# Three inner norms of a two-block kernel, with the sums of squares taken through a block of ones

## The chip, the core and the metric

The kernel runs on one core of a Trainium2 chip. The metric is device microseconds for one execution. TensorE (PE in the profile) multiplies, VectorE (DVE), ScalarE (ACT) and GpSimd (POOL) do the rest, and SyncE (SP) issues the transfers of the weights.

## The reference

256 tokens of width 1024 pass through two blocks. The first has two layers (a convolution beside a gated recurrence; then a multi-scale pooling mixer) and ends in a norm of its own; the second has two mixers side by side and a feed-forward part. Cut to the residual stream and its norms:

```python
def rmsnorm(x, g):   return x * rsqrt(mean(x * x) + 1e-6) * g
def modulate(h, shift, scale):   return h * (1 + scale) + shift

for l in (0, 1):                                        # first block
    h = modulate(rmsnorm(x, norm_g[l]), shift[l], scale[l])
    x = x + gate[l] * mixer[l](h)
x = rmsnorm(x, final_g)
h = modulate(rmsnorm(x, g_mix), mod[0], mod[1])         # second block
x = x + mod[2] * token_mixers(h)
h = modulate(rmsnorm(x, g_ffn), mod[3], mod[4])
x = x + mod[5] * swiglu(h)
return rmsnorm(x, g_final)
```

## The kernel before

The stream X is kept as [128 features, 8 feature tiles, 256 tokens], so a norm's sum over features runs over partitions and goes through TensorE. Every weight arrives as a piece of 128x2048 numbers (L330); ScalarE casts it to a high part (L309) and VectorE takes the low part (L310), and a product is three matmuls of 256 moving columns (L357 to L359). Modulation weights arrive in chunks (L502), of which some are multiplied by TensorE (L515, "w,S") and some by VectorE, whose partial sums `part` go through eight narrow matmuls (L482). Ten buffers of the pool `w` hold pieces and chunks. Instructions are put in order by a scheduler from priorities; ScalarE's table sets are loaded by `table` ahead of functions that need them, or where a function needs another set.

Three norms lie inside the kernel, each between a block's last product and the next block's first: **A** between layer 0 and layer 1, **B** between layer 1 and the second block (where two norms follow one another), and **C** between the mixers and the feed-forward part. At each, `residual` adds eight product tiles to X (L625) and squares X on ScalarE (L632, L637; at A and C in pairs that VectorE adds, L634). TensorE then sums the squares: the squares are the stationary operand, 128 tokens at a time, and one column of ones (at B two columns, ones and final_g squared) moves:

```python
for i in range(2):
    nc.tensor.matmul(ms[:, n * i:n * (i + 1)], s1[:, 128 * i:128 * (i + 1)],
                     ones[:, 0:1] if rhs is None else rhs[:, m, :], ...)
```

That leaves one number per token, by partition. `rstd_of` scales it on VectorE (L417) and raises it to -1/2 on GpSimd (L418); `spread` writes it on the diagonal of two 128x128 tiles (`dg`, L407 and L408) and multiplies these with ones (L411), so that all partitions hold the root of every token. Then `modulate` runs, per feature tile: `xa` on VectorE (L562), `h1h` on ScalarE (L563), `h1l` on VectorE (L564); at B the tiles are h2h and h2l, at C h4h and h4l.

At A and C, TensorE multiplies one weight piece with X scaled but not yet normed (`e1h`, `e1l`, `e4h`, `e4l`: L606, 48 matmuls of 258 columns), and VectorE multiplies these products with the root later; ScalarE copies the root out of its bank for that (`r`, L609). At B, products of the second context (`h2ch`, `h2cl`) stand there. At C, `HOLD` puts four matmuls of 256 columns, whose result nobody reads, between the sums (L653). The norm at the end of the kernel is already taken in another way (`wide`): ones are the stationary 128x128 block and the squares move, 256 columns at a time (L640), so that every partition gets the sum of every token; the root comes from Ln and Exp on ScalarE.

Of the kernel before, what the change touches and what calls it, by code (L numbers as in the profile page):

```python
# [28 lines left out]
HOLD = ((), (), (6, 6, 7, 7))  # L29
# [8 lines left out]
# Layer 0 after its first four pieces: weight pieces in order, with modulation chunks (md) between them; the  # L38
# convolution fills what they leave.
# [15 lines left out]
# Layer 1 likewise: (step, group, half).  # L55
# [7 lines left out]
# The mixers of block 2 likewise.  # L63
# [11 lines left out]
# The feed-forward: pairs of up projections, each pair's down projection one piece later.  # L75
# [11 lines left out]
P = 128  # L87
# [48 lines left out]
def pack(inp):  # L136
# [73 lines left out]
    # the convolution's taps in fours, [feature of 32, tap of four] by [feature tile, four, group of 32]  # L210
# [13 lines left out]
def build(tc, gates, wp, mp, vec, xT, cT, c2T, tok, cst, out, dbg=None):  # L224
# [54 lines left out]
    nc.vector.memset(eps6, 1e-6)  # L279
    mhalf = con.tile([P, 2], F32, name="mhalf")  # L280
# [34 lines left out]
    def halves(raw, width):  # L315
        """A weight piece's parts."""
# [27 lines left out]
    def piece(last=False):  # L344
        """The next weight piece; the ones after it are on their way (fewer behind the last of a layer)."""
# [15 lines left out]
    def mm_w(o, w, x, at, start, stop):  # L361
        """o += w[at].T @ x, in float32 (w and x whole) or in three float32r products of their parts."""
# [5 lines left out]
    def mm_cols(o, w, j, h):  # L368
        """o[128 columns, tokens] over all of D."""
# [3 lines left out]
    def cols2(pc, h):  # L373
        """Two column tiles in one bank."""
# [6 lines left out]
    def toks(o, w, h, s):  # L381
        """o[128 tokens, 256 columns] over all of D."""
# [6 lines left out]
    def mm_rows(banks, pc, x, first, last):  # L389
        """Adds two K tiles (x(k): parts) to all of the 1024 output columns."""  # L390
# [13 lines left out]
    def spread(col):  # L404
        """[128 tokens, 2] -> a bank's [128, 256], the same in all partitions."""
# [8 lines left out]
    def rstd_of(ms, n, eps):  # L414
        """(sum / n + eps) ** -0.5 of [128 tokens, 2] sums, spread over the partitions."""
# [15 lines left out]
    def warm(n):  # L431
        """Keeps the tensor engine's clock up while the first weights arrive."""
# [10 lines left out]
    def mod_part(k):  # L443
        """Shift and scale of layer 0, for 128 features (one mask, both conditions): partial sums by column tile."""
# [23 lines left out]
    def x_vector(block, c, w, part):  # L468
        """One block for x alone: two K tiles' products summed on the vector engine, the partitions' sums at the end."""
# [18 lines left out]
    def mod_groups():  # L488
        """Modulation vectors, a chunk at a time: [feature, column tile, condition] for one or two blocks of 1024 columns."""
# [84 lines left out]
    def token_sums(sums):  # L574
        """The sums over a tile's features, [128 tokens, 2]."""
# [5 lines left out]
    def sumsq_all(xs):  # L581
        """Sums of squares of eight feature tiles, in two tiles of four."""
# [10 lines left out]
    def shift_columns(h, sh):  # L593
        """The shift, as two more columns of the scaled X's parts."""
# [4 lines left out]
    def cols_early(pc, h, rs):  # L599
        """Column tiles from X scaled but not yet normed: [(products over the norm, their shift)]."""  # L600
# [7 lines left out]
        out, r = [], t1("r")  # L608
        nc.scalar.copy(r, rs)  # L609
        for b in banks:  # L610
            t, c = t1("t"), small("c", 1)
            nc.scalar.copy(c, b[:, T:T + 1])
            nc.vector.tensor_tensor(out=t, in0=b[:, 0:T], in1=r, op=ALU.mult)
# [3 lines left out]
    def residual(acc, gate, rhs=None, hold=(), early=None, wide=False):  # L617
# [3 lines left out]
        n = 1 if rhs is None else 2  # L621
        for m in range(8):
            pairs = rhs is None and m < 6
            with tc.high_priority():
# [4 lines left out]
                if pairs:  # L629
                    sq = t2("sq2", (P, 2, T))  # L630
                    s1 = sq if wide and m == 5 else t1("s1")
                    nc.scalar.activation(sq, X[:, m - 1:m + 1, :], AF.Square)  # L632
                    if not (wide and m == 5):
                        nc.vector.tensor_tensor(out=s1, in0=sq[:, 0, :], in1=sq[:, 1, :], op=ALU.add)  # L634
                else:
                    s1 = t1("s1")
                    tables["square"] = nc.scalar.activation(s1, X[:, m, :], AF.Square).ins  # L637
            if wide:
                for s in ([s1[:, 0, :], s1[:, 1, :]] if m == 5 else [s1]):
                    nc.tensor.matmul(ms[:, 0:T], ones, s, start=m == 1, stop=m == 7)  # L640
                continue
            for i in range(2):
                nc.tensor.matmul(ms[:, n * i:n * (i + 1)], s1[:, 128 * i:128 * (i + 1)], ones[:, 0:1] if rhs is None else rhs[:, m, :],
                                 start=m == (1 if rhs is None else 0) and i == 0, stop=m == 7 and i == 1)
# [6 lines left out]
        b = mm_bank()  # L651
        for m in hold:
            nc.tensor.matmul(b[:, 0:T], ones, X[:, m, :], start=True, stop=True)  # L653
        return ms

    lbm, om, omn, e0, e1 = (con.tile([P, 8], F32, name=n) for n in ("lbm", "om", "omn", "e0", "e1"))

    # ------------------------------------------------------------ layer 0
    with ExitStack() as st0:
# [61 lines left out]
        def half_piece(s, g, low):  # L721
            """The high or the low part of half of a piece."""
# [52 lines left out]
        # sigmoid(x) = (1 + tanh(x / 2)) / 2: half of the gates' biases and of the taps that follow one  # L775
# [3 lines left out]
        # 4 * softplus(-lam)  # L779
# [21 lines left out]
        # lower bounds of the forget gates: f = lb + om * (1 + tanh) = lbm + om * tanh  # L801
# [13 lines left out]
        # conv branch  # L815
# [9 lines left out]
        def parts(src):  # L825
            """Two feature tiles as the down projection takes them."""
# [4 lines left out]
        def glu(m, a, g):  # L831
            """Gated input of the convolution for one feature tile, and its taps, which give way to other work."""
# [6 lines left out]
        def shift(m):  # L839
            """[feature of 32, tap of four] on the partitions: a product has four taps."""  # L840
# [6 lines left out]
        def conv(m):  # L847
            """The convolution of one feature tile: its last taps on the tensor engine, the first on the vector engine."""
# [99 lines left out]
        def lru_out(m):  # L948
            """Scans and output gate of two heads; returns the gated output's parts."""
# [17 lines left out]
        def conv_norm():  # L967
            """Layernorm statistics of the conv branch."""
# [548 lines left out]
```

## Time and profile before

| | |
|---|---|
| time, median of 3 runs | 958.51 us (958.29 to 958.64) |
| span of the profiled execution, first to last instruction | 954.3 us |
| granted TensorE clock, mean over the span | 0.984 of full speed |
| TensorE busy | 97% |
| VectorE, ScalarE, GpSimd busy | 69%, 54%, 2% |
| HBM read | 182.23 MB, 192 GB/s over the span |

The profile gives no time of the profiled execution of its own beside the span, so 4.2 us of the median of the runs lie around the span. A busy TensorE can still be slow: the granted clock says at which of its two speeds it ran (1.00 is 2.4 GHz, 0.50 is 1.2 GHz), and the two must be read together.

### The profile page before, as it was taken

What the parts mean: (1) busy time and instruction counts of PE and PEld (TensorE: products, weight loads), DVE (VectorE), ACT (ScalarE), POOL (GpSimd) and SP (SyncE); (2) the same over time, 40 slices, a digit from 0 to 9 for tenths busy, and PEclk for the clock granted to TensorE, in tenths of its full rate; (3) what the DMA queues carried; (4) which work ended last, traced back from release to release, by engine and by line L of the source; (5) the groups of instructions that cost most, each with busy time, mean ns of one, the idle gap of its engine ahead of it and who ended that gap; (6) DMA issues with size and microseconds to landing.
All of it is one profiled execution on the core that took longest, in us unless ns stands there. A gap on an engine that the chain in (4) does not pass through costs nothing. (4 is left out here: it accounts for less than half of the span.)

```text
span 954.3 us, 18243 instructions
## 1 busy us (share of the span) xinstructions
PE 921.4 (97%) x7638; PEld 863.0 (90%) x7638; DVE 661.0 (69%) x1202; ACT 514.6 (54%) x929; POOL 16.7 (2%) x30
## 2 busy tenths in 40 slices
PE   8999999899978999999999999999999999999996
PEld 7876888696878789999999999899999999999996
DVE  4688787795786775878857344989578866555543
ACT  3454869677554454446543335872564663544442
POOL 0000000000000000000000000000000000000000
PEclk9999999999998899999989999999999999999999
DMA  9968573344665685564643363344746367555511
GB/s 367 408 205 308 177 251 112 116 177 177 225 222 211 234 298 183 208 230 178 256 153 136 136 220 139 140 158 178 264 147 251 133 220 255 188 180 181 194 65 45
DMA packets 31890, 189.11 MB, mean 198 GB/s; under 512 B 3552, under 2 KB 8032, under 8 KB 10688
## 3 DMA queue, kind: packets, MB, share of 16 engines
q1 hardware_dynamic: 31248, 185.46, 53.6%
q0 software_dynamic: 560, 2.49, 0.7%
q8 instruction: 60, 0.98, 0.4%
q14 instruction: 22, 0.18, 0.1%
HBM read 182.23 MB, written 1.05 MB: 192 GB/s over the span
## 5 line engine op out<-in xcount | busy, mean ns | idle before, releaser
L310 DVE TENSOR_TENSOR w<-w 128x512 fp32r<-128x512 f32 x460 | 297.8, 686 | 142.5 <-ACT w L309 97.3
L309 ACT CAST w<-w 128x512 fp32r<-128x512 f32 x460 | 255.5, 617 | 155.0 <-DVE w L310 103.8
L359 PE MATMUL mm<-h4h,w 128*128 128x256 f32 x336 | 94.7, 282 | 0.1
L358 PE MATMUL mm<-h4l,w 128*128 128x256 f32 x336 | 94.3, 281 | 0.0
L357 PE MATMUL mm<-h4h,w 128*128 128x256 f32 x336 | 94.2, 281 | 0.0
L358 PE MATMUL mm<-h2l,w 128*128 128x256 f32 x288 | 81.8, 285 | 0.0
L357 PE MATMUL mm<-h2h,w 128*128 128x256 f32 x288 | 81.6, 284 | 0.0
L359 PE MATMUL mm<-h2h,w 128*128 128x256 f32 x288 | 81.5, 284 | 0.0
L359 PE MATMUL mm<-hxh,w 128*128 128x256 f32 x256 | 73.1, 286 | 4.7 <-DVE w L310 4.7
L357 PE MATMUL mm<-hxh,w 128*128 128x256 f32 x256 | 72.7, 284 | 1.2 <-ACT w L309 1.2
L358 PE MATMUL mm<-hxl,w 128*128 128x256 f32 x256 | 72.2, 282 | 0.0
L359 PE MATMUL mm<-h1h,w 128*128 128x256 f32 x240 | 67.8, 283 | 0.0
L357 PE MATMUL mm<-h1h,w 128*128 128x256 f32 x240 | 67.7, 282 | 0.0
L358 PE MATMUL mm<-h1l,w 128*128 128x256 f32 x240 | 67.7, 282 | 0.0
L359 PEld LDWEIGHTS mm<-h4h,w 128*128 128x128 f32 x336 | 63.5, 189 | 0.3 <-DVE w L310 0.3
L358 PEld LDWEIGHTS mm<-h4l,w 128*128 128x128 f32 x336 | 63.4, 189 | 0.0
L357 PEld LDWEIGHTS mm<-h4h,w 128*128 128x128 f32 x336 | 63.2, 188 | 0.0
L358 PEld LDWEIGHTS mm<-h2l,w 128*128 128x128 f32 x288 | 54.3, 189 | 0.3 <-issue 0.2
L359 PEld LDWEIGHTS mm<-h2h,w 128*128 128x128 f32 x288 | 54.3, 189 | 0.2 <-issue 0.2
L357 PEld LDWEIGHTS mm<-h2h,w 128*128 128x128 f32 x288 | 54.3, 188 | 0.3
L357 PEld LDWEIGHTS mm<-hxh,w 128*128 128x128 f32 x256 | 48.2, 188 | 6.9 <-issue 3.8
L359 PEld LDWEIGHTS mm<-hxh,w 128*128 128x128 f32 x256 | 48.4, 189 | 6.6 <-DVE w L310 6.1
(398 smaller groups left out, 2513.0 us busy)
## 6 DMA issues: line engine op xcount, KB each, us to landing
w<-in_wp SPq DMA_DIRECT2D x115, 1024.0 KB, 4.9
w<-in_mp SPq DMA_DIRECT2D x48, 1024.0 KB, 5.4
four<-up SPq DMA_DIRECT2D x32, 142.0 KB, 3.9
w<-in_wp SPq DMA_DIRECT2D x8, 512.0 KB, 10.7
gw<-in_gates SPq DMA_DIRECT2D x4, 512.0 KB, 3.6
X<-in_xT SPq DMA_DIRECT2D x1, 1024.0 KB, 5.3
ct<-in_cT SPq DMA_DIRECT2D x2, 512.0 KB, 9.3
c<-in_c2T POOLq DMA_DIRECT2D x2, 512.0 KB, 6.3
```

The costliest lines, as they stand in the source:

```text
L309: a = nc.scalar.copy(hi, src).ins
L310: return a, nc.vector.tensor_tensor(out=lo, in0=src, in1=hi.bitcast(F32), op=ALU.subtract).ins
L357: nc.tensor.matmul(o, wh, xh, start=start, stop=False)
L358: nc.tensor.matmul(o, wh, xl, start=False, stop=False)
L359: nc.tensor.matmul(o, wl, xh, start=False, stop=stop)
```

## The change

All of `residual` takes the way of the last norm. Ones are stationary, the squares move, six matmuls of 256 columns per norm; the root comes out of `rstd_wide`, Ln and Exp on ScalarE, in all partitions, in SBUF. The narrow sums, GpSimd's power, the diagonals, `spread` at these places, the copy `r` and the four matmuls of `HOLD` go. At B the sums with the weight final_g squared come from squares of X scaled by its root (`weight`), one tile of 256 columns at a time, and the plain sums that the first of the two norms needs are taken apart, in `plain_sums`. Three `table` calls stand ahead of the residuals, and with the functions that follow them ScalarE has six more table loads in all.

```diff
-HOLD = ((), (), (6, 6, 7, 7))
+HOLD = ((), (), ())
...
-        out, r = [], t1("r")
-        nc.scalar.copy(r, rs)
+        out = []
...
-            nc.vector.tensor_tensor(out=t, in0=b[:, 0:T], in1=r, op=ALU.mult)
+            nc.vector.tensor_tensor(out=t, in0=b[:, 0:T], in1=rs, op=ALU.mult)
...
-                    nc.scalar.activation(sq, X[:, m - 1:m + 1, :], AF.Square)
-                    if not (wide and m == 5):
+                    if weight is None:
+                        nc.scalar.activation(sq, X[:, m - 1:m + 1, :], AF.Square)
+                    else:
+                        for j in range(2):
+                            nc.scalar.activation(sq[:, j, :], X[:, m - 1 + j, :], AF.Square, scale=weight[:, m - 1 + j:m + j])
+                    if m < 5:
...
-            if wide:
-                for s in ([s1[:, 0, :], s1[:, 1, :]] if m == 5 else [s1]):
-                    nc.tensor.matmul(ms[:, 0:T], ones, s, start=m == 1, stop=m == 7)
-                continue
-            for i in range(2):
-                nc.tensor.matmul(ms[:, n * i:n * (i + 1)], s1[:, 128 * i:128 * (i + 1)], ones[:, 0:1] if rhs is None else rhs[:, m, :],
-                                 start=m == (1 if rhs is None else 0) and i == 0, stop=m == 7 and i == 1)
+            for s in ([s1[:, 0, :], s1[:, 1, :]] if m == 5 else [s1]):
+                nc.tensor.matmul(o, ones, s, start=m == 1, stop=m == 7)
...
+    def plain_sums():
...
+        for i in range(4):
+            sq, s1 = t2("sq2", (P, 2, T)), t1("s1")
+            nc.scalar.activation(sq, X[:, 2 * i:2 * i + 2, :], AF.Square)
+            nc.vector.tensor_tensor(out=s1, in0=sq[:, 0, :], in1=sq[:, 1, :], op=ALU.add)
+            if i % 2:
+                nc.vector.tensor_tensor(out=s1, in0=s1, in1=sums.pop(), op=ALU.add)
+            sums.append(s1)
+        ms = ms_bank()
+        for i in range(2):
+            nc.tensor.matmul(ms[:, 0:T], ones, sums[i], start=i == 0, stop=i == 1)
+        return ms
+
+    def rstd_wide(ms, bias):
+
+        r = t1("rs")
+        act(r, ms[:, 0:T], AF.Ln, scale=1.0 / D, bias=bias)
+        act(r, r, AF.Exp, scale=-0.5)
+        return r
...
+        table("natural_log_exp_and_others")
         ms = residual(acc, mod_vector("gate0")[:, :, 0], hold=HOLD[0], early=early and (scale1, early))
...
-            rs1 = rstd_of(ms[:, 0:2], D, 1e-6)
...
+            rs1 = rstd_wide(ms, eps6)
...
+        nc.vector.tensor_tensor(out=fg2, in0=v("final_g", 0, 8), in1=v("final_g", 0, 8), op=ALU.mult)
+        nc.vector.tensor_scalar(out=fg2, in0=fg2, scalar1=1e-6, scalar2=None, op0=ALU.add)
+        nc.gpsimd.tensor_tensor(fg2, fg2, half, ALU.pow)
+        table("natural_log_exp_and_others")
...
-            nc.gpsimd.tensor_tensor(vb, vb, mhalf, ALU.pow)
-            rs3 = spread(vb)
-        nc.gpsimd.tensor_tensor(r2, va, mhalf, ALU.pow)
-        rs2 = spread(r2)
+            rs3 = rstd_wide(ms, eps12)
+        rs2 = rstd_wide(plain_sums(), eps6)
```

TensorE's order at norm A, from the last product of layer 0 (`acc<-yh,w`) to the first products of layer 1 (`mm<-h1h,w`); before, the narrow sums (`ms<-ones,s`) stand between early products, and the spread (`ms<-dg`) and the narrow matmuls of `part` behind them:

```order
L359 MATMUL acc<-yh,w 128x256
L643 MATMUL ms<-ones,s_3286 128x1 x2
L606 MATMUL acc<-e1h,w 128x258
L643 MATMUL ms<-ones,s_3294 128x1 x2
L606 MATMUL acc<-e1h,w 128x258 x13
...
L606 MATMUL acc<-e1h,w 128x258 x7
L411 MATMUL ms<-dg,ones 128x128 x2
L482 MATMUL ms<-ones,part 128x1 x8
L606 MATMUL acc<-e1h,w 128x258 x11
L606 MATMUL acc<-e1l,w 128x258 x14
```

Of the same place after the change:

```order
L361 MATMUL acc<-yh,w 128x256
L646 MATMUL ms<-s_3289,ones 128x256
...
L646 MATMUL ms<-s_3311,ones 128x256
L484 MATMUL ms<-ones,part 128x1 x8
L608 MATMUL acc<-e1h,w 128x258 x4
L517 MATMUL ms<-w,S_81 32x512 x12
L608 MATMUL acc<-e1h,w 128x258 x2
L517 MATMUL ms<-w,S_81 32x512 x4
L608 MATMUL acc<-e1h,w 128x258 x10
L525 MATMUL ms<-C,row 128x4 x4
L608 MATMUL acc<-e1h,w 128x258 x8
```

All six sums now stand together behind the last product, the eight narrow matmuls of `part` right behind them, and the modulation chunks (L515 before, L517 now), which stood behind all early products, between these.

TensorE's order at norm B, from layer 1's last product (`acc<-zh,w`) into the second context's products (`mm<-h2ch,w`), before:

```order
L359 MATMUL acc<-zh,w 128x256
L643 MATMUL ms<-fg_5410,s_5415 128x2 x2
L643 MATMUL ms<-fg_5410,s_5420 128x2 x2
...
L643 MATMUL ms<-fg_5410,s_5435 128x2 x2
L357 MATMUL mm<-h2ch,w 128x256
L358 MATMUL mm<-h2cl,w 128x256
```

And after:

```order
L361 MATMUL acc<-zh,w 128x256
L646 MATMUL ms<-s_5409,ones 128x256
L646 MATMUL ms<-s_5417,ones 128x256
L646 MATMUL ms<-sq_5424,ones 128x256 x2
L359 MATMUL mm<-h2ch,w 128x256
L646 MATMUL ms<-s_5430,ones 128x256
L646 MATMUL ms<-s_5434,ones 128x256
```

Ten narrow matmuls of the first five tiles stood together (six more follow between context products); now the six wide ones stand there with one context product among them, and the two of the plain sums come 16 and 23 context products later.

ScalarE's order at B after the change, from the squares scaled by `fg` to the first modulated tile (`h2h`); before, eight squares and no other work of the norm stood here but two diagonals:

```order
L638 ACTIVATE sq_5424<-X,fg_5398 128x256 x2
L664 ACTIVATE sq_5440<-X 128x512
L664 ACTIVATE sq_5444<-X 128x512
L644 ACTIVATE s_5430<-X,fg_5398 128x256
L644 ACTIVATE s_5434<-X,fg_5398 128x256
L664 ACTIVATE sq_5449<-X 128x512
L664 ACTIVATE sq_5453<-X 128x512
L294 ACTIVATE rs<-ms,eps_76 128x256
L311 CAST w<-w 128x512
L294 ACTIVATE rs<-rs 128x256
```

Two of the four plain squares come ahead of the last two weighted ones, and two between these and the Ln that reads their sum.

## Rows read from the trace of the kernel before

**Rows 1.** The page: TensorE's busy time, and its granted clock in 40 slices.

```profile
PE 921.4 (97%) x7638; PEld 863.0 (90%) x7638; DVE 661.0 (69%) x1202; ACT 514.6 (54%) x929; POOL 16.7 (2%) x30
PEclk9999999999998899999989999999999999999999
```

**Rows 2.** Stretches: us; busy PE, PEld, DVE, ACT, POOL; clock, DMA share, GB/s.

```profile
306.00:314.00 8.00, 8.00 (x70) 8.00 (x70) 5.92 (x16) 5.68 (x13) 0.34 (x1) 1.00 1.01 424
314.00:324.00 10.00, 9.16 (x50) 8.78 (x48) 7.51 (x19) 5.35 (x12) 0.52 (x1) 0.66 0.39 163
492.00:504.00 12.00, 12.00 (x65) 12.00 (x65) 3.95 (x10) 3.36 (x8) 2.67 (x4) 0.57 0.25 88
746.00:758.00 12.00, 11.84 (x94) 11.43 (x93) 9.57 (x27) 8.11 (x21) 0.88 (x1) 1.00 0.25 93
944.00:947.00 3.00, 2.34 (x11) 1.71 (x9) 2.24 (x8) 2.22 (x6) 0.00 (x0) 1.00 0.00 0
580.00:590.00 10.00, 10.00 (x86) 10.00 (x86) 4.08 (x7) 4.34 (x8) 0.00 (x0) 1.00 0.32 111
590.00:630.00 40.00, 37.35 (x308) 35.77 (x308) 39.49 (x74) 35.61 (x59) 1.07 (x2) 1.00 0.36 131
```

**Rows 3.** Timeline of TensorE at A: start, us, operation, count, wait before.

```profile
309.41 0.50 PE L643 MATMUL ms<-ones,s 128*128 128x1 f32 x4
...
314.99 0.68 PE L411 MATMUL ms<-dg,ones 128*128 128x128 f32 x4 [0.66 <-DVE dg L407]
315.51 3.14 PE L482 MATMUL ms<-ones,part 128*128 128x1 f32 x16
...
324.62 3.64 PE L515 MATMUL ms<-w,S 128*32 128x512 f32 x32
...
331.21 0.36 PE L357 MATMUL mm<-h1h,w 128*128 128x256 f32 x1
```

**Rows 4.** Timelines of ScalarE, GpSimd and VectorE at A.

```profile
310.62 0.71 ACT L637 ACTIVATE s<-X 128x256 f32<-128x256 f32 x2
...
313.66 0.86 POOL L418 TENSOR_TENSOR rs<-rs,mhalf 128x2 f32<-128x2 f32 x1 [110.10 <-DVE rs L417]
...
315.71 1.26 DVE L562 SCALAR_TENSOR_TENSOR xa<-X,a,ms 128x256 f32<-128x256 f32 x3
```

**Rows 5.** Timelines of TensorE and ScalarE at B.

```profile
491.09 2.29 PE L643 MATMUL ms<-fg,s 128*128 128x2 f32 x20
...
511.71 0.28 PE L359 MATMUL mm<-h2h,w 128*128 128x256 f32 x1
...
492.43 0.81 ACT L637 ACTIVATE s<-X 128x256 f32<-128x256 f32 x2 [0.23 <-DVE X L625]
```

**Rows 6.** Timelines of TensorE and VectorE at C.

```profile
747.57 0.51 PE L643 MATMUL ms<-ones,s 128*128 128x1 f32 x4
...
756.25 2.09 PE L606 MATMUL acc<-e4l,w 128*128 128x258 f32 x16
...
754.69 1.26 DVE L562 SCALAR_TENSOR_TENSOR xa<-X,a,ms 128x256 f32<-128x256 f32 x3
```

**Rows 7.** Timelines of TensorE and ScalarE in the last norm.

```profile
944.45 1.03 PE L640 MATMUL ms<-sq,ones 128*128 128x256 f32 x4
...
945.32 1.03 PE L640 MATMUL ms<-s,ones 128*128 128x256 f32 x4
946.38 0.47 ACT L292 ACTIVATE rs<-ms,eps 128x256 f32<-128x256 f32 x1 [0.41 <-PE ms L640]
946.89 0.42 ACT L292 ACTIVATE rs<-rs 128x256 f32<-128x256 f32 x1
```

**Rows 8.** Timeline of TensorE elsewhere: narrow matmuls of another `part`.

```profile
687.68 1.62 PE L482 MATMUL ms<-ones,part 128*128 128x1 f32 x14
```

**Rows 9.** ScalarE's table loads, grouped, and the timeline around one.

```profile
L292 ACT ACT_TABLE_LOAD x22 | 28.2, 1283 | 1.1 <-DVE lx L1263 0.7
...
588.48 0.60 ACT L292 ACTIVATE sg<-mm 128x512 f32<-128x512 f32 x1 [1.05 <-PE mm L359]
```

More of the change, by code (lines that the diff above doesn't have):

```diff
@@ L279, in build @@
     nc.vector.memset(eps6, 1e-6)
+    eps12 = con.tile([P, 1], F32, name="eps12")
+    nc.vector.memset(eps12, 1e-12)
     mhalf = con.tile([P, 2], F32, name="mhalf")
@@ L612, in cols_early, with residual @@
             nc.scalar.copy(c, b[:, T:T + 1])
-            nc.vector.tensor_tensor(out=t, in0=b[:, 0:T], in1=r, op=ALU.mult)
+            nc.vector.tensor_tensor(out=t, in0=b[:, 0:T], in1=rs, op=ALU.mult)
             out.append((t, c))
         return out
-    def residual(acc, gate, rhs=None, hold=(), early=None, wide=False):
+    def residual(acc, gate, weight=None, hold=(), early=None):
         ms = ms_bank()
-        n = 1 if rhs is None else 2
+        o = ms[:, 0:T]
         for m in range(8):
-            pairs = rhs is None and m < 6
+            pairs = m < 6
             with tc.high_priority():
@@ L630, in residual @@
                     sq = t2("sq2", (P, 2, T))
-                    s1 = sq if wide and m == 5 else t1("s1")
-                    nc.scalar.activation(sq, X[:, m - 1:m + 1, :], AF.Square)
-                    if not (wide and m == 5):
+                    s1 = sq if m == 5 else t1("s1")
+                    if weight is None:
[4 more added lines that the diff above has]
+                    if m < 5:
                         nc.vector.tensor_tensor(out=s1, in0=sq[:, 0, :], in1=sq[:, 1, :], op=ALU.add)
@@ L636, in residual @@
                     s1 = t1("s1")
-                    tables["square"] = nc.scalar.activation(s1, X[:, m, :], AF.Square).ins
-            if wide:
-                for s in ([s1[:, 0, :], s1[:, 1, :]] if m == 5 else [s1]):
-                    nc.tensor.matmul(ms[:, 0:T], ones, s, start=m == 1, stop=m == 7)
-                continue
-            for i in range(2):
-                nc.tensor.matmul(ms[:, n * i:n * (i + 1)], s1[:, 128 * i:128 * (i + 1)], ones[:, 0:1] if rhs is None else rhs[:, m, :],
-                                 start=m == (1 if rhs is None else 0) and i == 0, stop=m == 7 and i == 1)
+                    kw = {} if weight is None else {"scale": weight[:, m:m + 1]}
+                    tables["square"] = nc.scalar.activation(s1, X[:, m, :], AF.Square, **kw).ins
+            for s in ([s1[:, 0, :], s1[:, 1, :]] if m == 5 else [s1]):
+                nc.tensor.matmul(o, ones, s, start=m == 1, stop=m == 7)
         if early:
@@ L650, in residual @@
                                                in1=h[0][:, m, 0:T].bitcast(F32), op0=ALU.mult, op1=ALU.subtract)
-        b = mm_bank()
-        for m in hold:
-            nc.tensor.matmul(b[:, 0:T], ones, X[:, m, :], start=True, stop=True)
-        return ms
+        if hold:
+            b = mm_bank()
+            for m in hold:
+                nc.tensor.matmul(b[:, 0:T], ones, X[:, m, :], start=True, stop=True)
+        return ms
+    def plain_sums():
+        sums = []
+        for i in range(4):
[14 more added lines that the diff above has]
+        return r
     lbm, om, omn, e0, e1 = (con.tile([P, 8], F32, name=n) for n in ("lbm", "om", "omn", "e0", "e1"))
@@ L1152, in build @@
         nc.vector.tensor_tensor(out=fgA, in0=fgA, in1=v("final_g", 0, 8), op=ALU.mult)
-        fg2 = con.tile([P, KT, 2], F32, name="fg2")
-        nc.vector.memset(fg2, 1.0)
-        nc.vector.tensor_tensor(out=fg2[:, :, 1], in0=v("final_g", 0, 8), in1=v("final_g", 0, 8), op=ALU.mult)
+        fg2 = con.tile([P, KT], F32, name="fg2")
+        half = con.tile([P, KT], F32, name="half")
+        nc.vector.memset(half, 0.5)
+        nc.vector.tensor_tensor(out=fg2, in0=v("final_g", 0, 8), in1=v("final_g", 0, 8), op=ALU.mult)
+        nc.vector.tensor_scalar(out=fg2, in0=fg2, scalar1=1e-6, scalar2=None, op0=ALU.add)
+        nc.gpsimd.tensor_tensor(fg2, fg2, half, ALU.pow)
+        table("natural_log_exp_and_others")
         ms = residual(acc, mod_vector("gate1")[:, :, 0], fg2, HOLD[1])
@@ L1158, in build @@
         tap("x2", X)
-        mv = ms[:, 0:4].rearrange("p (i n) -> p i n", n=2)
-        va, vb, r2 = small("va"), small("vb"), small("r2")
-        nc.vector.tensor_scalar(out=va, in0=mv[:, :, 0], scalar1=1.0 / D, scalar2=1e-6, op0=ALU.mult, op1=ALU.add)
-        nc.vector.tensor_scalar(out=vb, in0=va, scalar1=1e-6, scalar2=None, op0=ALU.mult)
-        nc.vector.scalar_tensor_tensor(out=vb, in0=mv[:, :, 1], scalar=1.0 / D, in1=vb, op0=ALU.mult, op1=ALU.add)
         with tc.high_priority():
-            nc.gpsimd.tensor_tensor(vb, vb, mhalf, ALU.pow)
-            rs3 = spread(vb)
-        nc.gpsimd.tensor_tensor(r2, va, mhalf, ALU.pow)
-        rs2 = spread(r2)
+            rs3 = rstd_wide(ms, eps12)
+        rs2 = rstd_wide(plain_sums(), eps6)
         hx = [h_tile("h2h", "hxh"), h_tile("h2l", "hxl")]
@@ L1445, in build @@
             shift_columns(early, shift3)
+        table("natural_log_exp_and_others")
         ms = residual(acc, gate2, hold=HOLD[2], early=early and (scale3, early))
@@ L1448, in build @@
         with tc.high_priority():
-            rs4 = rstd_of(ms[:, 0:2], D, 1e-6)
+            rs4 = rstd_wide(ms, eps6)
     hx = [h_tile("h4h", "hxh"), h_tile("h4l", "hxl")]
@@ L1480, in build @@
     table("natural_log_exp_and_others")
-    ms = residual(acc, mod_vector("gate3")[:, :, 0], wide=True)
-    rs5 = t1("rs5")
+    ms = residual(acc, mod_vector("gate3")[:, :, 0])
     with tc.high_priority():
-        act(rs5, ms[:, 0:T], AF.Ln, scale=1.0 / D, bias=eps6)
-        act(rs5, rs5, AF.Exp, scale=-0.5)
+        rs5 = rstd_wide(ms, eps6)
     for m in range(8):
```

## The prediction

> **What bounds the kernel now.** I read the page first, then the busy time and clock by stretch, then the timelines of the three norms. The page says that TensorE is busy 97% of the span [rows 1], so time can come from three sources only: work that TensorE no longer does, moments in which it waits, and stretches in which it is busy at a lower clock. The clock line of the page shows 8 in place of 9 in two pairs of slices, around 310 and around 490 us [rows 1]. The stretches put numbers on them. At A the clock is 1.00 until 314 and 0.66 on the mean of the ten microseconds after it; at B it is 0.57 on the mean of the twelve from 492 [rows 2]. These are losses that busy shares hide: at B TensorE counts as busy for 12.00 of 12.00 us. At C the clock stays at 1.00 [rows 2].
>
> What did TensorE do before each fall? At B, twenty records of matmuls with two moving columns from 491.09 on, 2.2 us of them and nothing else, and the clock is down behind them [rows 2, 5]. At A, narrow sums among early products, a wait of 0.66 us for the diagonals, then sixteen records with one column, already slow at 3.14 us [rows 3]; fourteen of the same kind take 1.62 elsewhere [rows 8]. At C the narrow sums alternate with products, four of them kept for that. So what stands before a fall is narrow work by itself, with or without a wait. Narrow matmuls count as busy but do little.
>
> **The change, norm by norm.** I place TensorE's list of instructions after the change at full clock, add the waits, and compare the ends. Prices of one record or matmul: 0.13 us for an early product (16 in 2.09) [rows 6], 0.12 for a product of 256 columns (86 in 10 us) [rows 2], 0.43 for a wide sum (two in 0.87, since each has two records) [rows 7], 0.115 for a narrow one (14 in 1.62) [rows 8], 0.114 for one of a modulation chunk (32 in 3.64) [rows 3].
>
> A. The last product ends at 309.41 [rows 3]. Six wide sums: 2.6 us, to 312.0. The last square is done at 310.62 + 0.71 = 311.33 [rows 4], before the sixth sum would start, so no wait. Then sixteen records for `part`, 1.85, to 313.9. Then all that stands ahead of layer 1's products: 48 early products, 6.2; forty chunk records, 4.55; eight small ones for the chunks' rows, at the same price 0.9. That ends at 325.6. Before, these products run steadily from 331.21 on [rows 3], with nine of them done earlier, which is 330.1 if they had all been behind. Gain: 4.5 us. The parts bear it out: clock (1 - 0.66) x 10 = 3.4, idle 10 - 9.16 = 0.84 [rows 2]; the sums themselves and the diagonals make the rest. Can the norm keep up? Before, the power ends at 314.52, and `xa` starts at 315.71 [rows 4]. After, Ln and Exp end about 1.0 us behind the sums (0.47 and 0.42 with small gaps [rows 7]), at 313.0; `xa` waits a little longer, because the gate vector from `part` is ahead of it on VectorE, until about 314.1. Sixteen VectorE operations at 0.4 us then end near 321, ahead of 325.6. The chunks that now come earlier in TensorE's order are the other thing late: the queue is full until 314 (DMA share 1.01) and at 0.39 on the mean of the ten after that [rows 2], and the first chunk is wanted at 314.4. I take no wait; by one transfer's time, up to 2.5 us (1 MB at 424 GB/s), could go here. A gives between 1.0 (the dip stays) and 4.8; I take 4.5.
>
> B. From 491.09 to the end of the last product of the first two pieces at 511.83 it takes 20.7 us [rows 5]. After: 96 products at 0.12 make 11.5, eight wide sums 3.5, together 15.0. Waits: squares with a scale per column can't be paired, as they were not before either, but two plain squares stand ahead of the last two. These were done at 492.43 + 0.81 = 493.24 [rows 5]; two squares of double length, about 1.4 us by the rate of two in 0.71 [rows 4], less casts that moved, put them near 494.0, where TensorE wants them at 493.4. I add 0.9 us for that and for the second plain sum. End: 507.0, gain 4.8. The clock alone is (1 - 0.57) x 12 = 5.2 [rows 2]; the wide sums cost a little less than the narrow ones and the diagonals, and the new waits take more back. The norm: Ln at about 495.5 behind the last plain squares, Exp done by 497, `xa` from 497.1 instead of 504.1; sixteen VectorE operations and a few weight splits end by 505.5, ahead of the last products at 506.3. Bounds: 5.7 without waits; -0.4 where the dip stays.
>
> C. From 747.57 six wide sums, 2.6, then 48 early products, 6.24: 756.4, and 0.2 of waiting for the last squares, 756.6. Before, the last early product ends at 756.25 + 1.95 = 758.2 [rows 6]. Gain 1.6. `xa` starts at 754.69 before [rows 6]; it will start about 2.4 us earlier, so a few tenths of waiting for modulated tiles go too: I take 1.7, with 1.6 to 2.1 as bounds. No dip is there to win.
>
> **Table loads.** Six more, 1.28 us each (28.2 for 22) [rows 9], 7.7 us of ScalarE. Five are hidden by TensorE's own work: those ahead of the squares at A, B and C run while TensorE still multiplies the block's last pieces, those before layer 1's first gate and before the second block's first forget gates while it multiplies the piece that these read or the next. Without that cover each costs its 1.28. One is on a path: before `sg` at 588.48 ScalarE idles 1.05 [rows 9], so the load pushes it by 0.23, into a stretch in which VectorE is busy 39.49 of 40 us and TensorE 37.35 [rows 2]. I charge 0.2; uncovered, all six would cost 7.7. The Trainium skill ("ScalarE: Activation LUTs", section "What ACT_TABLE_LOAD costs") puts a switch at about 2.66 us with a drain beside the load; by it six switches would be 16 us. The trace has 1283 ns for the load itself [rows 9], and I go by that.
>
> Sum: 4.5 + 4.8 + 1.7 - 0.2 = 10.8. The span of 954.3 becomes 943.5; with the 4.2 us around it that the median shows, 947.7.
>
> **The rivals.**
>
> One dip stays. At A the narrow records of `part` stand right behind the sums, alone, as in the rows before a fall. At 687.68 the same kind ran at full speed, which speaks against it [rows 8]. Price 3.4: 951.1. At B new waits of 0.9 us stand among the sums; price 5.2: 952.9. The Trainium skill ("TensorE: Matmul & The Clock Gate", section "Why this matters for your kernels") blames idle gaps between bursts of matmuls for such falls. At B before no gap shows, 12.00 of 12.00 us are busy, and the clock fell all the same [rows 2]; by that rule narrow matmuls aren't the cause, the change removes no cause at B and even adds a gap, and the time is this rival's 952.9.
>
> Wide sums lower the clock as narrow ones did, at all three norms. This ends on the other side: A gives 1.1, B -0.4, and C, where the kept products are gone, gets a dip that it doesn't have, 3.4 to 5.2, against its 1.7. With the load's 0.2 that is a loss of 1.2 to 3.0: 959.7 to 961.5. It decides from a dip at C of 2.2 us on. Against it: in the last norm, with waits between wide sums (2.34 busy of 3.00), the clock shows 1.00 [rows 2].
>
> Table loads are on the path after all, each at its 1.28: 947.7 + 7.5 = 955.2. Against it: ScalarE is busy 54% [rows 1].
>
> The gain is given back further down: if VectorE's full stretch from 590 to 630 ended when it does now, A and B would be worth nothing and the time 957.0. But VectorE is busy 4.08 of the 10 us ahead of it [rows 2], so the stretch starts when TensorE brings its products, and moves with them.
>
> **How the numbers follow.** Forecast 0.62; one dip stays 0.17; three dips 0.06; loads 0.06; given back 0.05; 0.04 for what I don't see. The forecast's own range is 945 to 950 (the bounds of the three norms, and one late chunk). The range of 944.5 to 955.5 takes in one dip and the loads, and leaves out some 0.15. Faster or slower by 0.2%, 1.9 us, is about what a measurement of this kernel can tell from no change. Faster: forecast, one dip, most of the loads, part of the rest, 0.87. Within: given back, 0.05. Slower: three dips and unseen things, 0.08.
>
> **What would show it.** The clock at 1.00 through 305 to 325, and through a stretch of 20 us from about 486 on; layer 1's products steady near 325.6 on a clock of before, and B's end some 9 us earlier than 511.8; wide sums at 0.43 each; Ln right behind the sixth; `xa` at C near 752 less the shift. A time over 950 with the clock at 1.00 would mean waits that I haven't placed, for chunks at A or for ScalarE at B; a clock under 1.00 at any of the three would show narrowness was not the cause, or not alone.

## The result, and the profile after

The changed kernel takes 944.7 us (median of 4 runs, 941.7 to 946.9) against 958.4 us before (4 runs, 956.5 to 958.6); ratio 0.9865, 95% interval 0.9837 to 0.9893. Measured a second time it was 944.7 against 954.8 us (0.9891, 0.9867 to 0.9916). The ratios are given as recorded; the quotient of two medians differs from them a little (0.9857 in the first measurement). The prediction was 947.7 us, 944.5 to 955.5, so the measured time lies 0.2 us above the lower end of its range. The two gains, 13.7 and 10.2 us, are the same measurement twice, and the difference between them is a part of the story: the times of the kernel before go from 951.0 to 957.9 us in the second measurement, at mean clocks of 0.991 to 0.980 of full speed, and those of the changed kernel from 943.4 to 945.8 at 0.992 to 0.988. One of the five runs of the kernel with a fill, below, took 1475.6 us at a mean clock of 0.555 and is left out of that kernel's times.

The page of the changed kernel, TensorE's busy time and its clock, answers to [rows 1]:

```profile
PE 909.1 (97%) x7582; PEld 851.2 (91%) x7582; DVE 660.4 (70%) x1201; ACT 525.6 (56%) x941; POOL 15.0 (2%) x27
PEclk9999999999998999999999999999999999999998
```

One of the two low places, near 490 us, is gone. The other has shrunk to one slice, which belongs to something else, at 288 us. The 8 in the last slice stands where TensorE has no work left. Stretches of the changed kernel (columns as in [rows 2]):

```profile
306.00:314.00 8.00, 8.00 (x60) 6.02 (x62) 7.08 (x20) 6.18 (x15) 0.00 (x0) 1.00 1.01 422
314.00:324.00 10.00, 10.00 (x85) 6.93 (x74) 8.29 (x21) 7.01 (x15) 0.00 (x0) 1.00 0.56 193
484.00:500.00 16.00, 16.00 (x120) 15.21 (x119) 14.56 (x36) 13.72 (x30) 0.99 (x2) 1.00 0.19 67
735.00:747.00 12.00, 12.00 (x92) 11.54 (x91) 12.00 (x31) 11.53 (x29) 0.00 (x0) 1.00 0.26 87
282.00:288.00 6.00, 1.18 (x8) 0.98 (x6) 4.36 (x8) 5.73 (x12) 0.00 (x0) 0.84 0.71 269
288.00:296.00 8.00, 8.00 (x50) 7.99 (x50) 3.53 (x7) 5.06 (x8) 0.00 (x0) 0.69 0.00 0
```

The first two rows are A, the third B, the fourth C: TensorE is busy all the time and at full clock, where before it was at 0.66 and 0.57 behind A and B [rows 2]. The last two rows show a wait ahead of A, for the conv branch, and the dip behind it (a stretch at a low clock), which the change doesn't touch.

TensorE's timeline at A, B and C, with the rows that answer to [rows 3], [rows 5] and [rows 6]:

```profile
307.22 1.12 PE L646 MATMUL ms<-s,ones 128*128 128x256 f32 x4
...
309.20 1.14 PE L646 MATMUL ms<-s,ones 128*128 128x256 f32 x4
310.18 1.84 PE L484 MATMUL ms<-ones,part 128*128 128x1 f32 x16
...
484.80 1.02 PE L646 MATMUL ms<-s,ones 128*128 128x256 f32 x4
485.66 1.03 PE L646 MATMUL ms<-sq,ones 128*128 128x256 f32 x4
486.74 1.13 PE L646 MATMUL ms<-s,ones 128*128 128x256 f32 x4
489.63 0.59 PE L671 MATMUL ms<-s,ones 128*128 128x256 f32 x2
...
500.37 0.39 PE L387 MATMUL mm<-w,h2h 128*128 128x256 f32 x1 [0.27 <-ACT kx L294]
...
735.58 1.02 PE L646 MATMUL ms<-s,ones 128*128 128x256 f32 x4
...
737.30 1.05 PE L646 MATMUL ms<-s,ones 128*128 128x256 f32 x4
738.01 4.22 PE L608 MATMUL acc<-e4h,w 128*128 128x258 f32 x32
742.06 2.08 PE L608 MATMUL acc<-e4l,w 128*128 128x258 f32 x16
```

The sums follow the last product without a wait at all three; the row at 500.37 is the first behind the products that end B. The chain of the norm at A, on ScalarE and VectorE, and the last weighted squares at B:

```profile
310.38 0.47 ACT L294 ACTIVATE rs<-ms,eps 128x256 f32<-128x256 f32 x1 [0.39 <-PE ms L646]
310.88 0.42 ACT L294 ACTIVATE rs<-rs 128x256 f32<-128x256 f32 x1
...
312.06 0.17 DVE L486 TENSOR_TENSOR gate<-ms,V 128x8 f32<-128x8 f32 x1 [0.92 <-PE ms L484]
312.14 1.26 DVE L564 SCALAR_TENSOR_TENSOR xa<-X,a,rs 128x256 f32<-128x256 f32 x3
...
486.19 0.89 ACT L644 ACTIVATE s<-X,fg 128x256 f32<-128x256 f32 x2
```

The root is there 1.1 us behind the sums; `xa` waits 0.8 us more for the gate vector ahead of it on VectorE, as foreseen, and nothing waits for `xa`.

For all comparisons below, the length of a norm runs from the end of the block's last product (0.12 us behind the start of its last record) to a point behind it with the same number of products done: at A the start of the fortieth record of layer 1's products, at B the end of the first two pieces, at C the start of the sixtieth record of the feed-forward's. "Dip" is the loss of a stretch at a low clock: the sum of (1 - clock) times length over stretches of 4 us. Each kernel was profiled in one execution (the changed kernel in two). The ratio is to the kernel before, measured beside it; the kernel before has a median from each of the two measurements.

| kernel | A, us | B, us | C, us | dips at A, B, C, us | median, us | ratio to before |
|---|---|---|---|---|---|---|
| before | 25.4 | 20.7 | 18.0 | 3.4, 5.1, 0 | 958.4; 954.8 | |
| changed | 21.3 | 15.1 | 15.5 | 0, 0, 0 | 944.7 | 0.9865 |
| changed, again | 21.0 | 15.1 | 15.5 | 0, 0, 0 | 944.7 | 0.9891 |
| A alone | 21.0 | 19.3 | 18.0 | 0, 3.4, 0 | 950.6 | 0.9961 |
| B alone | 25.3 | 15.1 | 18.0 | 3.4, 0, 0 | 952.1 | 0.9962 |
| C alone | 25.4 | 20.8 | 15.5 | 3.4, 5.1, 0 | 951.7 | 0.9965 |

Between the norms nothing changed: from A to B 156.2 us in every row of this table, from B to C 235.4 to 235.7.

### The profile page after: what moved, and what is told of

It is laid out like the page before. It is cut to its first block, busy times and chain, and to the rows that moved or that the text cites. A ratio compares the mean times of both kernels' runs of the same rounds, so it can differ in the third digit from the quotient of the medians.

```text
span 939.6 us, 18146 instructions
## 1 busy us (share of the span) xinstructions
PE 909.1 (97%) x7582; PEld 851.2 (91%) x7582; DVE 660.4 (70%) x1201; ACT 525.6 (56%) x941; POOL 15.0 (2%) x27
## 4 chain that ended last, share of the span: by engine, by line
PE 83%; DVE 7%; ACT 6%; DMA 2%; issue 1%; SPq 0%; POOL 0%; DVEq 0%; ACTq 0%; POOLq 0%
PE mm L359 16%; PE mm L361 16%; PE mm L360 16%; PE acc L359 7%; PE acc L360 6%; PE acc L361 6%; PE acc L762 2%; PE ms L517 2%; PE acc L884 2%; PE acc L608 1%; ACT L294 1%; PE ms L646 1%; DVE w L312 1%; ACT w L311 1%; DMA w<-in_wp 1%
## 6 DMA issues: line engine op xcount, KB each, us to landing
w<-in_wp SPq DMA_DIRECT2D x8, 512.0 KB, 10.8
```

## The experiments

**The changed kernel again, and one norm at a time.** Four kernels on one chip. In three of them the sums, the root and their use at two of the norms are put back as they were; for "A alone":

```diff
-        table("natural_log_exp_and_others")
-        ms = residual(acc, mod_vector("gate1")[:, :, 0], fg2, HOLD[1])
+        ms = residual_n(acc, mod_vector("gate1")[:, :, 0], fg2, HOLD[1])
...
-            rs3 = rstd_wide(ms, eps12)
-        rs2 = rstd_wide(plain_sums(), eps6)
+            nc.gpsimd.tensor_tensor(vb, vb, mhalf, ALU.pow)
+            rs3 = spread(vb)
...
-            rs4 = rstd_wide(ms, eps6)
+            rs4 = rstd_of(ms[:, 0:2], D, 1e-6)
```

(`residual_n` is `residual` of the kernel before.)

> The changed kernel once more, for the spread of its times. The theory (the sums no longer lower the clock at A and B) expects the granted clock at 1.00 through all three norms in this execution too, and places the spread of 941.7 to 946.9 us outside the norms: in a dip that comes or stays away where TensorE idles for some microseconds (near 172 and 286 us). The rival (one dip stays in some executions, behind the narrow matmuls of part at A or the waits among the sums at B) expects, in a slow-ish execution, a clock under 1.00 between 306 and 324 or between 484 and 500 us. Time 942 to 947.

> The change at norm A alone. Theory: clock 1.00 at A, 0.57 still at B, A worth 3.9 to 4.5 us, the time 0.40 to 0.47% under before. Rival (the clock is lost by idle moments, not by narrow work): only the wait for the diagonals goes, A worth about 1 us.

> The change at norm B alone. Theory: clock 1.00 at B, 0.66 still at A, B worth 4.8 to 5.5 us, 0.50 to 0.58% under before. Rival (idle moments): B had no idle moment before and has some now, so the dip stays and B is worth 0.7 us at most.

> The change at norm C alone, where the clock was at 1.00 before. Theory: 1.7 to 2.2 us from the kept products and the shorter chain, 0.18 to 0.23% under before, dips at A and B as before. Rival (wide sums lower the clock too, once the kept products are gone): a dip behind 747 us and no gain.

Stretches around the norms, first of the changed kernel again (A, then B):

```profile
306.00:324.00 18.00, 18.00 (x140) 13.49 (x140) 16.69 (x44) 14.04 (x31) 0.00 (x0) 1.00 0.86 347
484.00:504.00 20.00, 19.73 (x151) 18.85 (x150) 18.57 (x45) 16.80 (x37) 0.99 (x2) 1.00 0.28 95
```

A alone (A, then B):

```profile
309.00:325.00 16.00, 16.00 (x124) 11.56 (x122) 13.95 (x36) 11.47 (x26) 0.00 (x0) 1.00 0.75 303
488.00:500.00 12.00, 12.00 (x77) 11.98 (x78) 5.35 (x15) 4.30 (x10) 2.68 (x4) 0.72 0.23 85
```

B alone (A, then B):

```profile
316.00:328.00 12.00, 11.12 (x70) 9.51 (x72) 9.83 (x24) 6.37 (x16) 0.30 (x1) 0.72 0.31 128
492.00:508.00 16.00, 16.00 (x120) 15.12 (x118) 14.57 (x36) 13.73 (x30) 0.99 (x2) 1.00 0.19 66
```

C alone (A, B, C):

```profile
316.00:324.00 8.00, 8.00 (x43) 8.00 (x44) 6.12 (x16) 4.05 (x9) 0.00 (x0) 0.57 0.35 145
492.00:508.00 16.00, 16.00 (x100) 15.98 (x99) 7.73 (x19) 6.19 (x15) 2.68 (x4) 0.68 0.19 66
745.00:760.00 15.00, 15.00 (x117) 14.55 (x116) 15.00 (x38) 14.55 (x34) 0.00 (x0) 1.00 0.32 120
```

The clock is at 1.00 at a norm where the sums are wide, and under it at A and B where they are narrow, without an exception in these profiles. The single gains by median, 4.3, 2.8 and 3.1 us (by ratio 3.7, 3.6 and 3.3, each within some 1.9), add up to the whole within their intervals, so no dependence between the norms shows. In the profiled executions A gives 4.1 to 4.5, B 4.1 to 5.6 and C 2.5 us. Part of the expectations missed. B alone came out 0.38% under before instead of 0.50 to 0.58, and C alone 0.35 instead of 0.18 to 0.23, each with an interval of some 0.2 either way. The clock's "0.57" at B is 0.72 over its stretch of 12 us in A alone, because the dip there cost 3.4 and not 5.1 us. So the dips at the same narrow sums differ between executions, and with them the gain. The rival that blames idle moments alone falls with B alone: no wait stood there before, and the dip is gone. At A the change takes away two things at once, narrow sums and a wait of 0.66 us for the diagonals [rows 3]; which of them brought the dip there was not tested apart.

**Does narrow work bring a dip?** Ten narrow matmuls, twenty records of two columns as before at B, whose result nobody reads, were put into the changed kernel, first ahead of the sums at B, then behind them; then twenty ahead of them; then ten in the middle of the feed-forward.

```diff
+            if weight is not None and m == 1:
+                fill = mm_bank()
+                for j in range(10):
+                    nc.tensor.matmul(fill[:, 2 * j:2 * j + 2], s1[:, 0:128], ones[:, 0:2], start=True, stop=True)
             for s in ([s1[:, 0, :], s1[:, 1, :]] if m == 5 else [s1]):
```

(Behind the sums: the same lines after this loop, with `m == 7`. Twenty: `range(20)`. In the feed-forward: with X as the stationary block, behind the ninth piece's products.)

> The changed kernel, with ten narrow matmuls (twenty records of two columns, 2.2 us, result unread) ahead of the first wide sum at B; they lie partly in moments in which TensorE waits there. Theory: the dip of 3.4 to 5.1 us comes back behind them, B takes 19 to 22 us instead of 15.1, and the time is 0.4 to 0.7% over the changed kernel. Rival (idle moments, not narrow work): B takes 16 to 17.3 us, 0.1 to 0.2% over.

Ahead of the sums, the row of the train and the stretch with all of B:

```profile
485.78 2.29 PE L648 MATMUL mm<-ones,s 128*128 128x2 f32 x20
...
485.00:504.00 19.00, 19.00 (x147) 18.45 (x147) 15.97 (x39) 14.57 (x32) 1.05 (x2) 1.00 0.16 56
```

No dip: B takes 17.5 us, 2.3 more than 15.1, which is the train itself; 946.8 us, ratio 0.9907 (0.9890 to 0.9925). The theory as I had put it, that narrow work by itself lowers the clock, missed here.

> The changed kernel with the ten narrow matmuls (twenty records of two columns, 2.2 us, result unread) behind the last wide sum at B, so that context products of 256 columns follow them, as in the kernel before; ahead of the sums they had brought no dip. Theory in its first form (narrow work of 2.2 us by itself lowers the clock, and wide sums behind it had hidden that): the clock falls behind them, B takes 15.1 + 2.2 + 3.4 to 5.1 = 20.7 to 22.4 us, 0.6 to 0.8% over the changed kernel. Rival (a train of this length alone is not enough): B takes 17.3 us, 0.2% over.

Behind the sums:

```profile
490.20 2.29 PE L650 MATMUL mm<-ones,s 128*128 128x2 f32 x20
...
487.00:505.00 18.00, 17.89 (x136) 16.86 (x135) 14.56 (x35) 13.52 (x30) 0.98 (x2) 1.00 0.17 59
```

Again none: B 17.5 us, 947.0 us, ratio 0.9923 (0.9893 to 0.9952). In these two profiles a train of 2.2 us beside wide sums cost about its own length and no more.

> The changed kernel with twenty narrow matmuls (forty records, 4.3 us) in place of ten ahead of the first wide sum at B. Theory in a weaker form (narrow work lowers the clock, but it takes more of it than 2.2 us when wide sums follow): a dip at B of 1.7 to 5.1 us, B 21 to 24.5 us, 0.6 to 1.0% over the changed kernel. Rival (narrow matmuls do not lower the clock at all): B 19.4 us, 0.45% over, the clock at 1.00.

Twice as long, ahead of the sums:

```profile
488.72 5.38 PE L648 MATMUL mm<-ones,s 128*128 128x2 f32 x40
...
488.00:500.00 12.00, 12.00 (x68) 10.99 (x67) 4.75 (x11) 4.72 (x11) 1.05 (x2) 0.72 0.25 89
```

Here the dip is back, 3.4 us, with TensorE busy for 12.00 of 12.00 us; B takes 23.0 us and the run 951.3 (0.9982, 0.9957 to 1.0006). The train alone takes 5.38 us where two of 2.29 would be 4.58, so the clock fell while it ran. So narrow work does lower the clock, without any wait, and forty records did at this place what twenty did not.

> The changed kernel with the ten narrow matmuls (twenty records of two columns, 2.2 us, one stationary block, result unread) in the middle of the feed-forward products, far from any wide sum: products of 256 columns on both sides, as around the narrow sums of the kernel before at B. Beside the wide sums such a train had brought no dip. Theory (a train of 2.2 us lowers the clock among products; the wide sums of twice the time per column beside it had held it up): a dip of 1.7 to 5.1 us behind it, 3.9 to 7.3 us or 0.4 to 0.8% over the changed kernel. Rival (such a train is not enough wherever it stands, and something else of the sums at B brought the dip there): 2.2 us, 0.23% over, the clock at 1.00.

Ten in the feed-forward, the train and the two stretches behind it:

```profile
817.47 2.29 PE L1497 MATMUL ms<-ones,X 128*128 128x2 f32 x20
...
818.00:822.00 4.00, 4.00 (x31) 4.00 (x31) 2.77 (x6) 1.61 (x5) 0.00 (x0) 0.85 0.76 264
822.00:826.00 4.00, 4.00 (x28) 4.00 (x27) 0.00 (x0) 1.02 (x2) 0.00 (x0) 0.72 0.00 0
```

A dip, but a short one: (1 - 0.85) x 4 + (1 - 0.72) x 4 = 1.7 us. The median is 948.1 us, ratio 0.9907 (0.9886 to 0.9929), with single times from 943.8 to 948.7; in this kernel C also took 1.6 us longer, in part because TensorE waited for VectorE among the sums there (0.28 and 0.56 us). Among products the same ten matmuls can bring a dip that they did not bring beside wide sums. One profile and six times don't say how often. One difference between all these trains and the sums of the kernel before stays untested: there, behind the twenty records, twelve more stand in three groups of four among the context products, inside the dip. The first group:

```profile
495.06 0.85 PE L643 MATMUL ms<-fg,s 128*128 128x2 f32 x4
```

**Wide work between the narrow sums.** The kernel before, with a wide matmul, unread, behind each of the first five narrow pairs at B:

```diff
+            if rhs is not None and m < 5:
+                if m == 0:
+                    fill = mm_bank()
+                nc.tensor.matmul(fill[:, 0:T], ones, X[:, m, :], start=True, stop=True)
```

> The kernel before, with five wide matmuls of 0.43 us, whose result nobody reads, one behind each of the first five pairs of narrow sums at B. Theory (narrow work by itself lowers the clock): the clock stays at 1.00 at B, so that B takes 20.7 - 5.1 + 2.2 = 17.8 us or a little more, with the extra work in it; the time is 0 to 0.3% under before. Rival (the narrow sums are not the cause): the dip stays, B takes 22.9 us and the time is 0.2% over before.

The stretch of B, the last narrow sums in it, and its one wait:

```profile
489.00:510.00 21.00, 19.81 (x161) 19.36 (x160) 15.28 (x38) 10.27 (x26) 2.68 (x4) 1.00 0.15 51
...
494.38 1.40 PE L643 MATMUL ms<-fg,s 128*128 128x2 f32 x12
...
498.87 1.16 PE L411 MATMUL ms<-dg,ones 128*128 128x128 f32 x8 [1.19 <-DVE dg L407]
```

The narrow sums are all still there, and the clock stays at 1.00. B takes 19.5 us, 1.2 less than before with 2.2 us of added work; 1.19 us go to the wait for the diagonals, which products at half the speed had hidden, as I read it. Twelve narrow records stand together even so, at 494.38, and bring no dip. The time stays the same (955.8 us, 1.0014, 0.9996 to 1.0032), not the 0 to 0.3% under before that I expected: in the profiled execution a dip of 3.4 us stood near 628 us, where none was before; whether the other eleven had it is not known. So at B of the kernel before the dip hangs on the twenty narrow records standing together, and the chain through GpSimd and the diagonals is the second price. What the whole kernel gains from parting them is not shown by this run.

**The kept products at C.** The kernel before with `HOLD = ((), (), ())`.

> The kernel before without its four kept products at C: ten narrow pairs there stand among early products by ones and twos only. If short trains are harmless (as at B of the changed kernel with ten narrow matmuls ahead): clock 1.00 at C, C 17.9 - 1.7 = 16.2 us or a little more where TensorE then waits, the time 0.1 to 0.2% under before. If the kept products held the clock: a dip of 1.7 to 3.4 us behind the sums, C 18 to 20 us, the time 0 to 0.2% over before.

```profile
744.00:764.00 20.00, 18.76 (x154) 18.19 (x153) 16.55 (x42) 14.78 (x34) 0.87 (x1) 1.00 0.22 68
```

The clock stays at 1.00 without them, C takes 17.6 instead of 18.0 us, and TensorE idles for 1.24 us of the twenty; 954.5 us, ratio 0.9994 (0.9971 to 1.0018). The kept products filled moments in which TensorE would have waited for the norm. At C the gain is thus mostly the chain: without a shorter chain, dropping them is worth 0.4 us of the 2.5 there, and nothing that shows in the whole time.

**Table loads on the path.** The changed kernel without its three `table` calls ahead of the residuals.

```diff
-        table("natural_log_exp_and_others")
         ms = residual(acc, mod_vector("gate1")[:, :, 0], fg2, HOLD[1])
```

> The changed kernel without its three table calls: the loads then stand right ahead of Ln and of Exp, in the chain of the norm (2.6 us more at A and C, 5.1 at B). Theory (at A and C the norm has slack behind the early products; at B it has little): A unchanged within 0.5 us, C 0 to 1 us longer, B 2 to 4 us longer, the time 0.2 to 0.5% over the changed kernel. Rival (the chain of the norm sets the end at all three): 10 us, 1.1% over.

ScalarE's loads at B, then TensorE's wait and its stretch:

```profile
493.68 1.28 ACT L294 ACT_TABLE_LOAD   x1
494.98 0.42 ACT L294 ACTIVATE rs<-rs 128x256 f32<-128x256 f32 x1
...
499.87 0.58 PE L359 MATMUL mm<-h2h,w 128*128 128x256 f32 x1 [3.96 <-ACT h2h L565]
...
496.00:508.00 12.00, 8.13 (x47) 8.13 (x48) 9.25 (x24) 6.79 (x12) 0.00 (x0) 0.72 0.00 0
```

In the profile A is unchanged (20.5), C 2.4 longer, B 6.7 longer (21.9); the median is 949.2 us, 0.9945 (0.9925 to 0.9964), half a per cent over the changed kernel. At A the loads hide behind the early products, as expected; at B four of them make TensorE wait 3.96 us, and with that wait the clock falls, which costs 3.4 more. Neither the theory's 2 to 4 us at B nor the rival's 10 us in all had this second part, and C missed the theory's 0 to 1 us. The profiled execution was the slowest of the six (953.4 us; four took 948.7 to 949.3), so the fall at B may not be in all of them.

**A fill for the wait ahead of A.** The changed kernel, with eight wide matmuls, unread, in the wait for the conv branch.

```diff
                 ga_piece(m)
+                if m == 3:
+                    fb = mm_bank()
+                    for i in range(8):
+                        nc.tensor.matmul(fb[:, 0:T], ones, gas[m][:, 0, :], start=True, stop=True)
```

> The changed kernel, with eight wide matmuls (3.5 us, result unread) where TensorE waits 4.8 us for the conv branch near 282 us, ahead of a dip that every profile shows. Theory (the clock follows what TensorE does; a wait of this length lowers it and wide work holds it): no dip behind 286 us, 3.4 us or 0.36% under the changed kernel. Rival (the fill only adds work, or the dip comes from elsewhere): the same time or up to 0.2% over.

The fill and the stretches that stand at 0.84 and 0.69 in the changed kernel, above:

```profile
285.80 3.72 PE L1054 MATMUL mm<-sa,ones 128*128 128x256 f32 x16 [0.87 <-ACT sa L294]
...
282.00:288.00 6.00, 5.13 (x35) 4.70 (x34) 5.17 (x10) 3.65 (x7) 0.00 (x0) 1.00 0.84 272
288.00:296.00 8.00, 7.77 (x58) 7.05 (x57) 3.96 (x8) 5.50 (x10) 0.00 (x0) 1.00 0.14 59
```

No dip at this place. The time is 941.5 us, ratio 0.9852 (0.9833 to 0.9871). That is 3.2 us under the changed kernel by the medians, nearly 4 us by the ratio of its second measurement (0.9891), and little over 1 us by that of its first (0.9865), whose interval holds it. So the dip is gone in the one profile; that this version is faster than the changed kernel is likely and not shown.

## Why the prediction was right, point by point

- **A, 4.5 us.** Measured 4.1 and 4.5 in two profiles. The parts were right: dip gone, idle gone, the norm's root with 1.1 us instead of about 1.0 behind the sums, `xa` held by the gate vector, the chunks in time. The wide sums cost 0.49 us each in the first profile instead of 0.43: (309.20 - 307.22) / 4. In the second they cost 0.43, and there the gain is 4.5.
- **B, 4.8 us.** Measured 5.6. The term that was off is the 0.9 us of waits: TensorE is busy 16.00 of 16.00 us there. I had the last weighted squares 2.9 us behind the last product; they are done 2.3 us behind it (486.19 + 0.89 - 484.80, in the last row of the norm's chain above), just when TensorE comes to them.
- **C, 1.7 us.** Measured 2.5, over my upper bound of 2.1. The terms that were off are the sums and the early products: these end 8.4 us behind the last product instead of 9.0, a gain of 2.2 instead of 1.6. The six sums take 2.43 us (735.58 to 738.01) instead of 2.6, the 48 early products 0.124 us each (738.01 to 743.98) instead of 0.13, and there is no wait for the last squares. The other 0.3 are the "few tenths" of waiting for modulated tiles.
- **Table loads, 0.2 us.** From B to C the time is 235.74 us before and 235.64 after, so the one load that I had on a path costs nothing that shows. The load and what stands behind it:

```profile
575.53 1.28 ACT L294 ACT_TABLE_LOAD   x1
576.82 0.60 ACT L294 ACTIVATE sg<-mm 128x512 f32<-128x512 f32 x1
```

  The 2.66 us that the Trainium skill ("ScalarE: Activation LUTs", section "What ACT_TABLE_LOAD costs") gives for a switch do not show here: the next function starts 0.01 us behind the load's 1.28, and the cast ahead of the load ends 0.02 us before it.
- **The start of the sum.** I put 4.2 us around the span, from the median of other runs. The result has a fourth time of the kernel before, 956.5 us; if it is that of the profiled execution, 2.2 us lie around its span of 954.3, as in twelve of the thirteen later profiles (1.8 to 2.1). With these the sum gives 945.7, and the rest to 944.7 is B and C, less what A fell short. The other way round, 2.2 us of the profiled difference are not the change's: layer 0's last product ends 2.2 us earlier in the profile after, of which 1.7 are a dip near 175 us that one execution has and the other not.
- **How near it was.** The terms held, and the number had some luck. Two of the four times, 941.7 and 942.8 us, lie under the range, and the median lies under the forecast's own 945 to 950. The profiles give 12.2 us for the three norms, against 10.8 in the sum; the first measurement has 13.7 and the second 10.2. Which dips an execution has, near 175 us and at B, can move the time by more than these differences, and the prediction had no term for it.
- **The clock line.** I read 8 in two pairs of slices. The line has one pair and a single 8 near 490 us [rows 1], and the first of the pair holds the dip near 288 us, which is not A's. The sum goes by the stretches [rows 2] and doesn't change.
- **The cause, "narrow work by itself".** Only partly right. The clock falls at A and B in every profile that has narrow sums there in their old order (five at A, four at B), and does not where wide matmuls stand in their place, or at B between them. But the same twenty records did not do it beside wide sums, so "2.2 us of narrow matmuls" is not a sufficient cause; forty records, or ten matmuls among products, brought a dip back. What exactly must surround them stays open.
- **The rivals.** One dip stays: in none of the six profiles with all three norms wide, their loads ahead of time and no train of forty records. Three dips with wide sums: no. Loads on the path: only without the `table` calls, and then 4.5 us. Given back further down: no, the stretch from B to C kept its length.
- The Trainium skill's rule ("TensorE: Matmul & The Clock Gate", section "Why this matters for your kernels"), that idle gaps between bursts bring the fall, agrees with the falls near 288 us, at a wait of 4.8 us, and in the kernel without `table` calls, at one of 3.96. At B before, and in the train of forty narrow records, the clock fell with TensorE busy all the time; there the measurement goes further than the rule.

## What to carry to other kernels

Read the granted clock beside the busy share, stretch by stretch: a TensorE at 100% can be at half its speed, and what it did just ahead of the fall is the place to look for the reason. Here that was narrow work at B and waits at 288 us. A sum over partitions through a block of ones with all tokens moving costs little more TensorE time than narrow sums (2.4 to 3.0 us for six here, against 2.3 us for twenty narrow records), gives the result in all partitions at once, and takes diagonals, a power on another engine and two hops out of the chain. Preload its tables: without that, C gave back 2.4 of its 2.5 us. Where a wait ahead of dense work can't be removed, unread wide matmuls in it can take the fall behind it away; whether they pay for themselves has to be measured.

## What the runs showed of the hardware

- The dips are not the same in each execution: at A 1.7 us (in the kernel with wide work between the sums at B) or 3.4, at B 3.4 or 5.1, and near 175 us none, 1.7 or 3.4 (before, changed and C alone: 1.7, 0, 3.4). The kernel before went from 951.0 us at a mean clock of 0.991 to 957.9 at 0.980 on one chip, so a single profile fixes the place of a loss and not its size.
- Beside wide float32 sums a train of twenty narrow records brought no dip in two kernels; among products of 256 columns it brought one of 1.7 us in the feed-forward. Each was profiled once, and that the wide sums are the reason is not shown.
- A wide sum took 0.49 us at A in the first profile of the changed kernel, with a DMA share of 1.01, and 0.43 at C, (737.30 - 735.58) / 4, with 0.26. The transfers are not the reason: in the second profile it took 0.43 at A too, (311.62 - 309.89) / 4, with the same share of 1.01. Why the first was slower stays open.

```profile
309.89 1.02 PE L646 MATMUL ms<-s,ones 128*128 128x256 f32 x4
...
311.62 1.03 PE L646 MATMUL ms<-s,ones 128*128 128x256 f32 x4
...
309.00:313.00 4.00, 4.00 (x27) 3.62 (x26) 4.00 (x12) 3.60 (x10) 0.00 (x0) 1.00 1.01 426
```
